# In-projection of a hybrid diffusion layer: TensorE keeps the order of the source instead of the scheduler's

## The chip, the cores and the metric

The kernel runs on one core of a Trainium2 chip. The metric is the time of one execution on the device in microseconds (us). The profile is one execution recorded by the hardware profiler; its times are counted from the first instruction of the program. PE is TensorE, DVE VectorE, ACT ScalarE, POOL GpSimd; SP is the queue that issues most DMA transfers. Each engine executes its own list of instructions strictly in the order of the program and waits on semaphores for the others.

## The reference

One layer of a backbone over 1024 latent tokens and 256 context tokens, width 1024, in float32. Cut to what matters:

```python
px = modulate(rms_norm(x, norm1_w), sh1, sc1) @ w_in       # latent, 1024 tokens
pc = modulate(rms_norm(ctx, norm1_w), csh1, csc1) @ w_in   # context, 256 tokens
# group A, gated DeltaNet on the first columns: short conv + SiLU on q, k, v; l2-normalised q, k;
# per chunk: decay, m = strict_lower((k beta) k^T * decay), a_mat = I + m, triangular solves with a_mat,
# then a scan over the chunks, forward and backward
# group B, neighbourhood attention: RMSNorm on q, k; 8 x 16 window keys and all context keys, one softmax
x = x + g1 * (concat([dn_x, na_x]) @ w_out)
x = x + g2 * swiglu(modulate(rms_norm(x, norm2_w), sh2, sc2), w_ffn_in, w_ffn_out)
```

The in-projection (`@ w_in`) with all that can already be done from its results (conv, norms, inverses of the chunks' triangular matrices) is the stage of this case. It lies at about 60 to 580 us of the span; attention and the scan follow up to about 815 us, then the output projection and the FFN.

## The kernel before

Every product with a large weight is taken in three passes of a split type: operands are divided into a high part (`whi`, `hh`) and a low part (`wlo`, `hl`), and high x high, high x low and low x high are summed in PSUM.

The stage works through a list of 24 **jobs**, each a block of 128 output columns for all tokens (`Block`, line 402, 8 k-tiles of 9 or 6 matmuls) or a wider one per token tile (`Wide`, lines 585 and 603, 24 matmuls a tile). The order of the jobs is k0, k1, k2, k3, z1, nk0, nk1, nk2, z0, nk3, nq0, nq1, nq2, q0, q1, q2, q3, nv0, v0, nv1, v1, v2, v3, nq3. (k, q, v, z belong to DeltaNet; nk, nq, nv to the neighbourhood attention.) k0 and k1 run before the loop that is changed.

The loop of lines 1032 to 1087 is a software pipeline written by hand. In turn n it issues the matmuls of job n; between them, step by step, the end of job n-2 (`finish`: transposes at line 524, products k k^T or q k^T at line 546); after them the copy of job n out of PSUM (`evac`: lines 435 to 458, with the convolution on DVE), the norm of job n-1 (`norm`: line 489 or 483) and the SiLU or square of job n. The weights of job n+1 are loaded at the start of turn n (line 195) and split by ACT (line 199) and POOL (line 200).

Beside that run two **background** generators, one step per k-tile or two per token tile:

- `block_inverses` (lines 806 to 892): decay tables (801), log-decays (837), 32 transposes to bring the 32 x 32 blocks on partitions (856), then on DVE 30 dependent pairs of multiply (866) and add (868) that invert all blocks in the tile `N`, then 32 transposes back (878) with copies by ACT (880), transposes and scalings on DVE (886, 889) and stores to `x_d` (888, 891).
- `preps` (898 to 1008): ten rounds, one for each position of the scan, each for both directions: decay products on POOL (`rg`, 938), matmuls 948 and 949, exp on ACT (952), products on DVE (955, 960), matmuls 967, copy 970, then three dependent steps of matmul 978 and copies on DVE (980) and ACT (981); diagonal blocks are copied by POOL (958, `y`) and ACT (942, `fx`) out of `xc`, which SP loads from `x_d` (922); results are stored by SP (990). Two rounds are in work at a time. The first two rounds are issued early; the other eight are issued once all q jobs are finished.

A third generator, `modulation` (lines 204 to 243), runs from job nq0 on and adds up the adaLN rows (232, 234) with four matmuls at line 219 for each of four parts. After job nv1, SP issues 64 transfers that rearrange the values (`vw_d`, line 1082).

What sets the order: the source only says in which order instructions are written. When the program is built, a scheduler decides for each engine, from a model of durations, which of the instructions that are ready in its model goes next, earlier written ones first; tiles get their buffers in the same pass. A block under `tc.manual_schedule(engines=...)` keeps the written order on the named engines; the other engines are still ordered by the scheduler. The kernel already has such a block for PE, DVE and ACT around the part before the loop.

Of the kernel before, what the change touches and what calls it, by code (L numbers as in the profile page):

```python
# [16 lines left out]
PSUM = bass.MemoryType.PSUM  # L17
DRAM = bass.MemoryType.DRAM

D, L, CT, T = 1024, 1024, 256, 1280  # L20
KT = 8
# [7 lines left out]
BLKS = [0, 8, 24, 32]  # L29
# [59 lines left out]
def hybrid(ctx, tc, a, dbg):  # L89
    nc = tc.nc  # L90
    pe, act, dve, pool, sp = nc.tensor, nc.scalar, nc.vector, nc.gpsimd, nc.sync

    def pools(stack, name, side=None, bufs=1, **kw):
        if side:
            kw["side"] = side
        return stack.enter_context(tc.tile_pool(name=name, bufs=bufs, reuse_waits="tile", **kw))
# [16 lines left out]
    middle = ctx.enter_context(ExitStack())  # L113
# [33 lines left out]
    nv_d = dram.tile([T, 512], F32, name="nv_d", tag="nv_d")  # L147
    nq_d = dram.tile([NAH, 2, ND, L], F16, name="nq_d", tag="nq_d")
    nk_d = dram.tile([2, NAH, ND, T], F16, name="nk_d", tag="nk_d")
    vw_d = dram.tile([128, 4, 4, 4, 128], F32, name="vw_d", tag="vw_d")  # L150
# [24 lines left out]
    bg = Background()  # L175
# [74 lines left out]
    attn = ctx.enter_context(ExitStack())  # L250
    psum = []
# [122 lines left out]
    with ExitStack() as bs:  # L374
# [4 lines left out]
        early = ExitStack()  # L379
# [362 lines left out]
        late = ExitStack()  # L742
# [153 lines left out]
        done = set()  # L896
# [113 lines left out]
        jobs = first + [Block("k", 2), Block("k", 3), Wide("z", 1, zp)]  # L1010
        inv = len(jobs)
        jobs += [Block("nk", i) for i in range(3)] + [Wide("z", 0, zp), Block("nk", 3)]
        jobs += [Block("nq", i) for i in range(3)] + [Block("q", 0)]
        turn = len(jobs)
        jobs += [Block("q", i) for i in (1, 2, 3)]
        later = len(jobs)
        values = later + 2
# [3 lines left out]
        def blk(n):  # L1021
            return jobs[n] if 0 <= n < len(jobs) and isinstance(jobs[n], Block) else None

        bg2 = Background()
# [4 lines left out]
        first[1].evac()  # L1029
        first[0].norm()  # L1030
        first[1].silu()
        for n in range(2, len(jobs) + 2):
            j = jobs[n] if n < len(jobs) else None
            if n == inv:
                early.close()
                psum.append(bs.enter_context(tc.tile_pool(name="psa", bufs=1, space=PSUM)))
                bg.add(block_inverses())
                bg.add(preps())
            if n == len(jobs) - 1:
                bg.drain()  # L1040
                bg2.drain()
                late.close()
                sp1 = pools(middle, "sp1", "left")
                fill = attention(pools(attn, "nw", "left", 2))
                next(fill)
            if n + 1 < len(jobs):
                jobs[n + 1].prefetch()
            fin = blk(n - 2) if n - 2 not in done else None
            fin = fin.finish() if fin else iter(())
            nrm = blk(n - 1)  # L1050
            if isinstance(j, Wide):
                for t, _ in enumerate(j.tiles()):
                    next(fin, 0)
                    if t == 4 and nrm:
                        nrm.norm()
                        for _ in fin:
                            pass
                        fin = nrm.finish()
                        done.add(n - 1)
                        nrm = None  # L1060
                    if n < turn:
                        bg.step(2)
                    if n >= turn:
                        bg.step(2)
            elif j:
                for k in range(KT):
                    j.mm([k])
                    if k >= 3:
                        next(fin, 0)
                    bg.step(1)  # L1070
                    if n > inv + 4:
                        bg2.step(1)
                j.evac()
            for _ in fin:
                pass
            done.add(n - 2)
            if isinstance(j, Wide) and n == values:
                vlat = nv_d[CT:].rearrange("(r c) d -> r c d", c=64)
                for cb in range(4):
                    for ch in range(4):  # L1080
                        for r in range(4):
                            sp.dma_start(vw_d[r * 32:r * 32 + 32, :, cb, ch],
                                         vlat[4 * ch + r, BLKS[cb]:BLKS[cb] + 32].rearrange("c (h d) -> c h d", d=128))
            if nrm:
                nrm.norm()
            if isinstance(j, Block):
                j.silu()

        dve.tensor_scalar(SQ, SQ, EPS, None, op0=OP.add)
        rsqrt(RQ, SQ, RQ2)  # L1090
# [226 lines left out]
    nrm = pools(early_u, "nrm", "left")  # L1317
# [11 lines left out]
    class Stream:  # L1329
# [67 lines left out]
        def next(self, n=2):  # L1397

            while len(self.got) < n:
                self.make()  # L1400
            out = [self.got.pop(0) for _ in range(n)]
            return out
# [21 lines left out]
    with ExitStack() as os_:  # L1424
        late = Background()
# [60 lines left out]
    with ExitStack() as us:  # L1486
# [91 lines left out]
        late = Background()  # L1578
# [170 lines left out]
```

## Time and profile before

| | us |
|---|---|
| time, median of 3 runs | 1555.27 (1553.62 to 1555.58) |
| time of the profiled execution | 1559.04 |
| its span, first to last instruction | 1556.6 |
| PE busy in the span | 1480.3 (95%) |
| PE busy from 60 to 580 us | 486.7 of 520 |

Busy time is a union of the times in which an engine's instructions ran. An engine can be busy and yet slow: the granted clock of PE is given separately. In a row of the timeline the columns are start, length, engine, line, operation, output and inputs with shapes, how many instructions were merged, and in brackets the idle time of the engine before it with what ended it. A matmul's length is its latency; in a stream the next one starts before it ends.

### The profile page before, as it was taken

To read this page: it belongs to the slowest core of one execution; us is meant where nothing else is said; L and a number is where in the kernel's file an instruction comes from. 1 tells how busy PE (TensorE), PEld (TensorE's weight loads), DVE (VectorE), ACT (ScalarE), POOL (GpSimd) and SP (SyncE) were. 2 spreads that over 40 slices of the span, in tenths; PEclk is the share of its full clock that TensorE was granted. 3 is DMA by queue.
4 is the path that set the end of the run, shared out by engine and by line. 5 is a ranking of instruction groups with operands and counts; after the bars stand their busy time and mean duration, and the time that the engine had idled before them with its cause. 6 is when DMAs were issued, how large, how long until landed. Compare 5 with 4: busy or idle time off the path is not lost. (4 is left out here: it accounts for less than half of the span.)

```text
span 1556.6 us, 23940 instructions
## 1 busy us (share of the span) xinstructions
PE 1480.3 (95%) x8702; PEld 1237.2 (79%) x8702; DVE 987.5 (63%) x1712; ACT 723.6 (46%) x1400; POOL 238.2 (15%) x286
## 2 busy tenths in 40 slices
PE   6999899999989987999899999999999999999998
PEld 3788787679888766887787878888888888888887
DVE  5774496674254755667786559856565656689652
ACT  5442553664343455665774256333333333454440
POOL 1154501633353320111210000000000000000000
PEclk9999999999999999999999999999999999999999
DMA  9274221677355568898737601633322224698742
GB/s 389 61 220 126 72 76 61 185 227 220 122 173 158 167 190 251 280 279 254 224 109 234 236 34 50 230 107 105 106 102 102 102 101 156 227 380 285 239 147 81
DMA packets 202423, 267.35 MB, mean 172 GB/s; under 512 B 16833, under 2 KB 112577, under 8 KB 201281
## 3 DMA queue, kind: packets, MB, share of 16 engines
q1 hardware_dynamic: 196688, 261.07, 51.5%
q10 hardware_dynamic: 5616, 4.76, 0.9%
q8 instruction: 68, 1.11, 0.3%
q14 instruction: 51, 0.41, 0.1%
HBM read 201.02 MB, written 68.94 MB: 173 GB/s over the span
## 5 line engine op out<-in xcount | busy, mean ns | idle before, releaser
L402 PE MATMUL blk<-hh,whi 128*128 128x512 f32 (+1 forms) x410 | 121.3, 390 | 1.4 <-ACT kk L547 1.4
L1387 ACT CAST uhi<-wq 128x512 fp32r<-128x512 f32 x101 | 61.0, 622 | 132.0 <-issue 84.6
L1387 ACT CAST uhi<-ws 128x512 fp32r<-128x512 f32 x91 | 53.9, 621 | 146.5 <-PE ps L1326 92.6
L402 PE MATMUL blk<-hh,wlo 128*128 128x512 f32 (+1 forms) x410 | 116.7, 378 | 0.6 <-POOL wlo L200 0.6
L402 PE MATMUL blk<-hl,whi 128*128 128x512 f32 (+1 forms) x410 | 115.6, 377 | 0.3 <-DVE hl L688 0.3
L1388 DVE TENSOR_TENSOR ulo<-wq,uhi 128x512 fp32r<-128x512 f32 x101 | 67.6, 688 | 58.8 <-ACT uhi L1387 32.5
L1326 PE MATMUL ps<-hT,uhi 128*128 128x512 f32 x336 | 103.6, 390 | 0.0
L1326 PE MATMUL ps<-lT,uhi 128*128 128x512 f32 x336 | 103.5, 389 | 0.0
L1326 PE MATMUL ps<-hT,ulo 128*128 128x512 f32 x336 | 103.5, 389 | 0.0
L1326 PE MATMUL ps<-hB,uhi 128*128 128x512 f32 x288 | 89.2, 391 | 0.6 <-ACT hB L1501 0.6
L1326 PE MATMUL ps<-lB,uhi 128*128 128x512 f32 x288 | 88.8, 389 | 0.4 <-DVE lB L1502 0.4
L1326 PE MATMUL ps<-hB,ulo 128*128 128x512 f32 x288 | 88.7, 389 | 0.0
L585 PE MATMUL blk<-zhi,hh 128*128 128x256 f32 (+1 forms) x288 | 84.5, 294 | 1.1 <-ACT kk L547 1.1
L402 PEld LDWEIGHTS blk<-hh,wlo 128*128 128x128 f32 x410 | 72.2, 191 | 15.4 <-POOL wlo L200 0.9
L402 PEld LDWEIGHTS blk<-hl,whi 128*128 128x128 f32 x410 | 72.4, 192 | 14.7 <-DVE hl L688 0.8
L585 PE MATMUL blk<-zhi,hl 128*128 128x256 f32 (+1 forms) x288 | 83.1, 288 | 0.0
L402 PEld LDWEIGHTS blk<-hh,whi 128*128 128x128 f32 x410 | 69.1, 191 | 16.4 <-issue 4.0
L585 PE MATMUL blk<-zlo,hh 128*128 128x256 f32 (+1 forms) x288 | 81.6, 283 | 0.0
L304 DVE CUSTOM_DVE_ANT_0 bt<-sc,bt 128x640 f32<-128x640 f32 x64 | 52.6, 822 | 34.6 <-PE sc L302 12.9
L1326 PEld LDWEIGHTS ps<-hT,ulo 128*128 128x128 f32 x336 | 63.1, 188 | 13.2
L1326 PEld LDWEIGHTS ps<-lT,uhi 128*128 128x128 f32 x336 | 63.1, 188 | 13.1
L1326 PEld LDWEIGHTS ps<-hT,uhi 128*128 128x128 f32 x336 | 62.9, 188 | 12.9
(360 smaller groups left out, 3645.9 us busy)
## 6 DMA issues: line engine op xcount, KB each, us to landing
wq<-w_fo SPq DMA_DIRECT2D x99, 256.0 KB, 4.3
wq<-w_gu SPq DMA_DIRECT2D x88, 256.0 KB, 2.8
wad<-wa SPq DMA_DIRECT2D x64, 256.0 KB, 3.9
bt<-rpb SPq DMA_DIRECT2D x64, 192.0 KB, 3.8
t_d<-g SPq DMA_DIRECT2D x22, 512.0 KB, 3.5
fr<-t_d SPq DMA_DIRECT2D x44, 256.0 KB, 5.1
f_d<-g SPq DMA_DIRECT2D x33, 256.0 KB, 2.1
fr<-f_d SPq DMA_DIRECT2D x33, 256.0 KB, 4.3
```

The source lines that it names most:

```text
L304: dve.tensor_tensor_reduce(bt, sc[:, u * 640:u * 640 + 640], bt, -1.0, 3.0e38, OP.add, OP.min, m[:, 0:1])
L402: pe.matmul(o, ww[:, k], xx[k][:, s], start=k == 0 and j == 0, stop=k == KT - 1 and j == 2)
L585: pe.matmul(p[:, :c1 - c0], x[k][:, s], ww[:, k, c0:c1], start=k == 0 and j == 0, stop=k == KT - 1 and j == 2)
L1326: pe.matmul(o, w[wi][:, k], x[xi][:, k], start=first and k == 0 and j == 0, stop=k == n - 1 and j == 2, skip_group_check=True)
L1387: act.copy(hi, self.raw[key])
L1388: dve.tensor_tensor(lo, self.raw[key], hi.bitcast(F32), OP.subtract)
```

## The change

The loop over the jobs is put under a manual schedule for PE. The body is the same, one level deeper, so line numbers behind line 1031 grow by one.

```diff
         first[1].silu()
-        for n in range(2, len(jobs) + 2):
-            j = jobs[n] if n < len(jobs) else None
-            if n == inv:
...
+        with tc.manual_schedule(engines={mybir.EngineType.PE}):
+            for n in range(2, len(jobs) + 2):
+                j = jobs[n] if n < len(jobs) else None
+                if n == inv:
...
+                if nrm:
+                    nrm.norm()
+                if isinstance(j, Block):
+                    j.silu()
```

The same instructions are issued, on the same tiles. On PE they stand in the written order inside the loop. ACT, DVE, POOL and SP are still ordered by the scheduler, now around a PE whose order is given.

More of the change, by code (lines that the diff above doesn't have):

```diff
@@ L1031, in hybrid @@
         first[1].silu()
-        for n in range(2, len(jobs) + 2):
-            j = jobs[n] if n < len(jobs) else None
-            if n == inv:
[L1035 to L1068, printed above, removed]
-                        next(fin, 0)
[L1070 to L1087, printed above, removed]
@@ new lines, in hybrid @@
+        with tc.manual_schedule(engines={mybir.EngineType.PE}):
+            for n in range(2, len(jobs) + 2):
+                j = jobs[n] if n < len(jobs) else None
+                if n == inv:
+                    early.close()
+                    psum.append(bs.enter_context(tc.tile_pool(name="psa", bufs=1, space=PSUM)))
+                    bg.add(block_inverses())
+                    bg.add(preps())
+                if n == len(jobs) - 1:
+                    bg.drain()
+                    bg2.drain()
+                    late.close()
+                    sp1 = pools(middle, "sp1", "left")
+                    fill = attention(pools(attn, "nw", "left", 2))
+                    next(fill)
+                if n + 1 < len(jobs):
+                    jobs[n + 1].prefetch()
+                fin = blk(n - 2) if n - 2 not in done else None
+                fin = fin.finish() if fin else iter(())
+                nrm = blk(n - 1)
+                if isinstance(j, Wide):
+                    for t, _ in enumerate(j.tiles()):
+                        next(fin, 0)
+                        if t == 4 and nrm:
+                            nrm.norm()
+                            for _ in fin:
+                                pass
+                            fin = nrm.finish()
+                            done.add(n - 1)
+                            nrm = None
+                        if n < turn:
+                            bg.step(2)
+                        if n >= turn:
+                            bg.step(2)
+                elif j:
+                    for k in range(KT):
+                        j.mm([k])
+                        if k >= 3:
+                            next(fin, 0)
+                        bg.step(1)
+                        if n > inv + 4:
+                            bg2.step(1)
+                    j.evac()
+                for _ in fin:
+                    pass
+                done.add(n - 2)
+                if isinstance(j, Wide) and n == values:
+                    vlat = nv_d[CT:].rearrange("(r c) d -> r c d", c=64)
+                    for cb in range(4):
+                        for ch in range(4):
+                            for r in range(4):
+                                sp.dma_start(vw_d[r * 32:r * 32 + 32, :, cb, ch],
+                                             vlat[4 * ch + r, BLKS[cb]:BLKS[cb] + 32].rearrange("c (h d) -> c h d", d=128))
+                if nrm:
+                    nrm.norm()
+                if isinstance(j, Block):
+                    j.silu()
```

## Prediction

> **What bounds the kernel now.** I read the page first: PE is busy for 95% of the span, and the stage that is changed is one of its less full parts. Then busy time of the engines in stretches of that stage, then who PE waited for in it.
>
> ```profile
> 60.00:224.80 164.80, 155.17 (x982) 135.57 (x981) 108.23 (x149) 80.38 (x138) 66.07 (x59) 1.00 0.39 120
> 224.80:255.80 31.00, 27.40 (x142) 22.84 (x140) 30.03 (x32) 6.49 (x10) 2.55 (x1) 0.99 0.18 52
> 255.80:311.50 55.70, 52.45 (x295) 39.41 (x295) 29.28 (x31) 35.21 (x63) 29.07 (x36) 0.88 0.51 164
> 311.50:400.00 88.50, 86.92 (x535) 76.74 (x534) 47.36 (x63) 41.42 (x61) 25.22 (x22) 0.98 0.68 201
> 400.00:513.70 113.70, 102.95 (x831) 90.67 (x830) 51.44 (x58) 48.08 (x106) 54.16 (x53) 0.97 0.52 159
> 513.70:533.10 19.40, 19.40 (x101) 16.24 (x99) 13.08 (x17) 4.50 (x6) 2.31 (x8) 1.00 0.82 265
> 533.10:565.00 31.90, 28.87 (x249) 21.87 (x249) 19.73 (x29) 17.94 (x40) 14.00 (x21) 1.00 0.31 105
> ```
>
> The columns are stretch, length, then busy time (instructions) of PE, PE's weight loads, DVE, ACT and POOL, then PE's granted clock, the share of the DMA engines and GB/s. PE fills most of each stretch, so what delays it there lengthens the kernel. One stretch is full on two engines: from 224.8 to 255.8, DVE is busy for 30.0 of 31.0 us while PE has 27.4 us of work. That DVE work is the inversion of the blocks in `N`:
>
> ```profile
> L868 DVE TENSOR_TENSOR N<-N,tt 80x120 f32<-80x120 f32 (+14 forms) x30 | 27.5, 916 | 0.9
> L866 DVE TENSOR_TENSOR tt<-N 80x120 f32<-80x120 f32 (+14 forms) x30 | 27.5, 915 | 4.7 <-ACT N L858 3.8
> L497 DVE SCALAR_TENSOR_TENSOR cacc<-cacc,qkw,cr 128x1280 f32<-128x1280 f32 x2 | 3.1, 1547 | 0.3 <-ACT cr L494 0.3
> L503 DVE TENSOR_TENSOR hl<-cacc,hl 128x1280 f16<-128x1280 f32 x2 | 3.0, 1480 | 0.0
> ```
>
> These groups of DVE, asked for 193.9 to 256.7 us, add up to 61 of 62.8 us: 30 dependent pairs back to back, with two norms between them. Nothing that PE does brings `N` forward. PE's waits from 60 to 580 us:
>
> ```profile
> PE pr L967 <- DVE y L980: 5.6, 3, 2.6
> PE pr L967 <- DVE kk L955: 4.8, 4, 3.8
> PE m L878 <- DVE N L872: 3.6, 1, 3.6
> PE pr L948 <- POOL rg L938: 3.2, 3, 1.8
> PE m L489 <- ACT cr L490: 2.9, 2, 1.5
> ```
>
> Each line is total, times and longest. All are small: the scheduler gave PE other matmuls while results of DVE and POOL were on their way.
>
> **The change, part by part.** The programs as built show how the order on PE moves. Around the transposes back out of `N` (line 878), rows of one kind merged by me:
>
> ```
> before: L585 x59 | L402 x116 | L878 x2 | L402 x3 | L878 x6 | L402 x4 | L878 x8 | L402 x2 | L878 x8 | L402 x2 | L878 x8 | L402 x4 | ...
> after:  L585 x48 | L878 x8 | L585 x24 | L878 x16 | L402 x9 | L878 x8 | L402 x36 | L948 x2 | L949 | L948 x2 | L949 | L402 x9 | L967 x8 | ...
> ```
>
> The scheduler had put 24 matmuls of z0 and 116 of nk3 and nq0 ahead of the first transpose; the source has it before them. The order of DVE's 60 inversion steps is the same in both.
>
> *A, the displaced work.* Where PE stands, what it did before the transpose, and when `N` is ready:
>
> ```profile
> 224.82 0.28 PE L585 MATMUL blk<-zhi,hh 128*128 128x264 f32 x1
> ...
> 227.72 0.74 PE L402 MATMUL blk<-hh,whi 128*128 128x256 f32 x3
> ```
> ```profile
> 226.50:252.20 25.70, 24.48 (x116) 20.04 (x116) 1.00 0.22 62
> ```
> ```profile
> 255.62 0.38 DVE L868 TENSOR_TENSOR N<-N,tt 80x232 f32<-80x232 f32 x1
> ```
> ```profile
> 255.83 0.53 PE L878 MATMUL m<-cst,N 80*128 80x80 f32 x2 [3.63 <-DVE N L872]
> 256.10 1.20 PE L402 MATMUL blk<-hl,whi 128*128 128x512 f32 x2
> ```
>
> After the change PE meets the transpose at 224.8 and stands still until `N` comes, about 29 to 31 us instead of 3.63. The matmuls behind it are ready (the next one ran 0.3 us after the transpose) but cannot pass. The work that filled the time, 27.4 us by the second row of the first table (2.9 us of z0, 24.5 of line 402), is still to be done. One thing comes back: POOL's split of a weight, which waits for PE to free a buffer, will not run beside the inversion. It did, and one DVE step took three times its neighbour:
>
> ```profile
> 242.57 2.55 POOL L200 TENSOR_TENSOR wlo<-wraw,whi 128x1024 fp32r<-128x1024 f32 x1 [40.88 <-ACT whi L199]
> ```
> ```profile
> 241.88 0.98 DVE L866 TENSOR_TENSOR tt<-N 80x792 f32<-80x792 f32 x1
> 242.89 3.07 DVE L868 TENSOR_TENSOR N<-N,tt 80x792 f32<-80x792 f32 x1
> ```
>
> 3.07 less 0.98 is 2.1 us. A is 27.4 - 2.1 = **+25.3** (25.3 to 27.4).
>
> *B, from `N` to the first two rounds of preps.* Before, this is how the chain went:
>
> ```profile
> 265.14 1.51 DVE L886 STREAM_TRANSPOSE ut<-WK 128x1280 f32<-128x1280 f32 x1 [8.51 <-ACT WK L880]
> ...
> 273.97 1.50 DVE L886 STREAM_TRANSPOSE ut<-WK 128x1280 f32<-128x1280 f32 x1
> ```
> ```profile
> 277.66 2.85 POOL L200 TENSOR_TENSOR wlo<-wraw,whi 128x1024 fp32r<-128x1024 f32 x1 [16.12 <-ACT whi L199]
> 280.46 0.99 POOL L912 MEMSET fx<- 128x512 f32 x2
> ...
> 284.29 1.03 POOL L938 TENSOR_TENSOR rg<-GL,cst 128x512 fp32r<-128x512 f32 x1
> ```
> ```profile
> 284.37 0.51 PE L948 MATMUL pr<-rg,mr 128*128 128x512 f32 x1 [1.83 <-POOL rg L938]
> ```
>
> The first matmul of the preps comes 28.5 us after the first transpose. Afterwards only 32 transposes (0.15 us apart), 24 z0 and 45 matmuls of line 402 lie between, about 4.8 + 2.9 + 9 us, so PE arrives some 17 us after `N`. The chain is shorter too: POOL's wlo and DVE's norms no longer stand in it. But the last transposes come later, behind 24 z0 and 9 others (4.7 us), and the stores that must land before `rg` gets its memory stay. I estimate `rg` at 24 us after `N` (not below 20, not over 28), a wait of 7. The whole stretch idled 3.25 us before (55.70 less 52.45). B is **+4** (0 to +8). What PE does in the wait's place is nothing; nk3 and nq0 then lie between the preps instead of nq1 and nq2.
>
> *C, the first turn.* In turn 2 the third bank and the first transposes were put off:
>
> ```profile
> 72.21 0.39 PE L402 MATMUL blk<-hl,whi 128*128 128x512 f32 x1
> ...
> 80.39 1.25 PE L524 MATMUL m<-cst,cacc 128*128 128x128 f32 x10
> ```
> ```profile
> 78.12 1.28 ACT L465 ACTIVATE cacc<-cacc 128x1280 f32<-128x1280 f32 x1
> ```
>
> In the written order PE waits at about 69 for the bank, which was in use at 72.21, and 34 matmuls of some 0.19 us later reaches the first transpose at about 78.5, 0.9 us before ACT's SiLU ends at 79.4. That is some 3 us lost, of which later waits on DVE and ACT (line 489 among them) swallow two. C is **+1** (0 to +3).
>
> *D, the rounds behind the 64 transfers.* Here the scheduler had put 98 matmuls of line 402 ahead of line 978:
>
> ```profile
> 486.95 29.73 SPq L1082 DMA_DIRECT2D vw_d<-nv_d  x46
> ```
> ```profile
> 520.49 2.67 POOL L958 COPY y<-xc 32x128 f32<-32x128 f32 x8 [9.11 <-DMA y_d<-y]
> ```
> ```profile
> 513.74 0.83 PE L402 MATMUL blk<-hh,whi 128*128 128x256 f32 x3
> ```
>
> SP issues one transfer in 0.65 us, so stores and loads of the preps queue behind them until 516.7, and POOL's copies end at 523.2. The written order has 18 matmuls (3.5 us) after 513.74 and then line 978: a wait from 517.2 to 523.2, 6.0 us at the same places. It is long enough to lower the clock (below), 3.4 us more. What the scheduler paid for the delay, 3.0 us idle from 533.1 to 565, goes. D is 6.0 + 3.4 - 3.0 = **+6.4** (0 to +9.4).
>
> *The clock.* After the 3.63 us of idle time:
>
> ```profile
> 252.00:256.00 4.00, 0.37 (x2) 0.17 (x2) 3.72 (x9) 0.00 (x0) 0.00 (x0) 0.89 0.00 0
> 256.00:260.00 4.00, 4.00 (x15) 3.22 (x16) 0.56 (x3) 2.20 (x4) 0.83 (x1) 0.50 0.00 0
> 260.00:264.00 4.00, 4.00 (x27) 3.58 (x26) 0.00 (x0) 2.70 (x6) 1.54 (x1) 0.76 0.24 71
> ```
>
> Lost clock: 4 x (0.11 + 0.50 + 0.24) = 3.4 us. A already pays one such drop before and one after, however long the wait, so it adds nothing there; B has one on both sides too. [...]
>
> *E, fewer changes of kind.* Three matmuls of line 402 take 0.09 us more behind line 967, which is in full float32, than behind line 585 (0.83 at 513.74, 0.74 at 227.72). By the built programs PE goes from one kind to another 42 times less. E is **-3** (-4 to 0). From 577 to 650 us the order on PE shifts by up to 50 places, behind that it is the same; ACT gets three more table loads beside other work. Both: 0 (-2 to +2).
>
> **The sum.** 25.3 + 4 + 1 + 6.4 - 3 = +33.7 us on the profiled execution of 1559.04 (span 1556.6), 1592.7. The median of the runs is 3.8 lower, so I predict **1589 us**.
>
> **The rivals.** *The lag is made up later.* PE idles 1.6, 10.8 and 3.0 us in the stretches from 311.5 to 400, 400 to 513.7 and 533.1 to 565. If the results waited for there come at fixed times, a late PE waits less. Against it: line 967 waits for products of line 955, which start from PE's own 948. All of it recovered is -15.4: 1574 us. Chance 0.14.
>
> *The other side: not slower.* That holds if the loop's second half is bound by the chain of the preps and not by PE, so that the displaced matmuls fall into its holes. Idle time after 255.8 is 3.3 + 15.4, lost clock 0.12 x 55.7 + 0.02 x 88.5 + 0.03 x 113.7 = 11.9: 30.6 us in all. It decides from 27.4 us recovered on; with all of it and without D and B the time is 1555.3 + 25.3 + 1 - 3 - 30.6 = 1548 us. Against it: the eight later rounds stand behind q3 in the written order, so their chain starts late with PE. Chance 0.04.
>
> *More waits.* Two rounds, not one, meet the transfers of line 1082, and the adaLN sums (line 219), which start 50 us later, are late as well: another 9.4 and some 5 us, 1603 us. Chance 0.10.
>
> *No effect* is excluded by the built order but for 0.01. My forecast has 0.71.
>
> **How the numbers follow.** The range is 1571 to 1604: the low end is the recovery, the high end the sum of the upper bounds (27.4 + 8 + 3 + 9.4 + 2 = 49.8, 1605) and the third rival. No change within 0.2% (3.1 us, about what a measurement can tell) has 0.02: slower by more than that 0.94, faster 0.04.
>
> **What would show it.** A: line 878 waits 28 to 31 us for `N`, in one piece, from about 225. B: line 948 waits 4 to 11 us near 273. D: line 978 waits for POOL's `y` near 550. The eight later rounds start about 30 us later than 410. I am wrong if `N` is ready much before 253, if PE passes line 878 sooner, or if the start of attention is not 25 to 45 us later than 579.

## The result, and the profile after

The changed kernel takes 1613.38 us (median of 4 runs, 1610.17 to 1617.19) against 1554.44 us of the kernel before on the same chip. The ratio is 1.0374, with a 95% interval of 1.0357 to 1.0391: it is slower by some 59 us, where 34 were predicted, and the time lies above the predicted range. The span of the profiled execution is 1612.8 us against 1556.6, and PE's mean granted clock 0.967 against 0.983.

First the busy time in stretches of the stage, in the columns used above. The stretches answer to those of before: where PE reaches the transposes, where it leaves them, and the later rounds of the preps.

```profile
60.00:240.00 180.00, 159.36 (x983) 138.06 (x981) 110.97 (x151) 83.56 (x140) 65.72 (x59) 0.96 0.36 110
240.00:265.90 25.90, 0.02 (x1) 0.05 (x1) 24.97 (x30) 0.64 (x2) 0.00 (x0) 0.60 0.14 36
265.90:340.00 74.10, 64.48 (x376) 50.93 (x377) 19.58 (x23) 32.70 (x64) 31.85 (x52) 0.89 0.42 135
340.00:444.00 104.00, 103.30 (x592) 88.92 (x591) 53.80 (x71) 49.98 (x66) 18.02 (x7) 0.97 0.56 169
444.00:557.00 113.00, 101.87 (x825) 89.75 (x823) 48.10 (x53) 47.47 (x105) 52.92 (x53) 0.95 0.51 157
557.00:637.00 80.00, 63.07 (x414) 50.08 (x413) 42.54 (x58) 30.72 (x54) 18.39 (x34) 0.89 0.50 157
```

From 240.0 to 265.9 PE has no work at all beside DVE's inversion. That is the wait that the prediction's step A named. But two more stretches lose time. To the same place in the work (983 instructions of PE against 982) PE needs 180.0 us from 60 on, where it needed 164.8: 15 us are gone before the wait begins. And the last stretch has 17 us of idle time at a clock of 0.89. PE's waits from 60 to 660 us (total, times, longest) say for whom:

```profile
PE m L878 <- DVE N L872: 25.9, 1, 25.9
PE m L489 <- ACT cr L490: 13.0, 4, 7.4
PE pr L978 <- DVE y L980: 12.5, 4, 5.3
PE pr L948 <- POOL rg L938: 6.0, 3, 5.6
PE pr L967 <- DVE kk L955: 5.4, 3, 4.5
PE pr L978 <- POOL y L958: 4.6, 2, 4.0
```

The longest ones in PE's timeline, in order of time:

```profile
188.46 2.08 PE L489 MATMUL m<-cr,cst 128*128 128x512 f32 x2 [7.35 <-ACT cr L490]
...
265.88 0.51 PE L878 MATMUL m<-cst,N 80*128 80x80 f32 x2 [25.92 <-DVE N L872]
...
290.15 0.80 PE L948 MATMUL pr<-rg,mr 128*128 128x512 f32 x1 [5.63 <-POOL rg L938]
...
568.20 0.78 PE L978 MATMUL pr<-y,kk 128*32 128x32 f32 x16 [4.04 <-POOL y L958]
...
596.60 1.07 PE L978 MATMUL pr<-y,kk 128*32 128x64 f32 x16 [3.47 <-DVE y L980]
...
617.94 1.49 PE L978 MATMUL pr<-y,kk 128*32 128x96 f32 x16 [5.27 <-DVE y L980]
```

Lines 878, 948 and 978 (for POOL's `y`) are the waits of steps A, B and D. The first row, and the two waits of line 978 for DVE, stand in no step of the prediction; a third wait of line 978 for DVE, 3.42 us, ends at 491.31.

How late the kernel is at four marks puts a size on each place:

| mark | before, us | after, us | later by |
|---|---|---|---|
| first step of DVE's inversion (line 866) | 193.98 | 205.02 | 11.0 |
| first matmul of nv0 (line 585) | 372.61 | 416.78 | 44.2 |
| last norm of the stage (line 489) | 576.52 | 635.92 | 59.4 |
| end of the span | 1556.6 | 1612.8 | 56.2 |

So 11 us are lost before the inversion starts, 33 from there to nv0, and 15 in the late turns; attention and what follows give 3 back. (PE itself is 15 us late at line 878, because it also waits 2.35 and 1.34 us at line 489 while the inversion runs; `N` is what it waits for next, so these two cost nothing more.)

**What stood in front of the inversion.** ACT's timeline of the changed kernel, around 184 us:

```profile
177.25 0.38 ACT L839 ACTIVATE W<-m 128x256 f32<-128x256 f32 x1
184.32 1.05 ACT L199 CAST whi<-wraw 128x1024 fp32r<-128x1024 f32 x1 [6.69 <-DMA wraw<-w_nqk]
185.27 1.35 ACT L435 ACTIVATE cacc<-blk 128x256 f32<-128x256 f32 x3
186.64 1.28 ACT L490 ACT_TABLE_LOAD   x1
187.93 1.05 ACT L490 ACTIVATE cr<-m,bias 128x256 f32<-128x256 f32 x2
```

and of the kernel before, at the same work:

```profile
174.47 0.38 ACT L839 ACTIVATE W<-m 128x256 f32<-128x256 f32 x1
176.81 1.36 ACT L435 ACTIVATE cacc<-blk 128x256 f32<-128x256 f32 x3 [1.96 <-PE blk L402]
178.19 1.28 ACT L490 ACT_TABLE_LOAD   x1
...
182.16 1.05 ACT L199 CAST whi<-wraw 128x1024 fp32r<-128x1024 f32 x1
```

The change does not touch ACT. But the scheduler, which orders ACT around a PE whose order is now given, put the cast of the next weights (line 199) ahead of the copy out of PSUM (line 435) and of the norm (line 490). The cast has to wait for its weights: SP issued that load at 179.92, and ACT stood still for 6.69 us with work behind the cast that was ready (PE's last matmul for the copies of line 435 ended at 179.82). The norm came at 187.93 instead of 179.49, PE waited for it, and the whole chain to `N` started late. In these rows the copies behind the cast did not pass it: it starts at 184.32, they at 185.27.

### The profile page after: what moved, and what is told of

Its sections match the earlier page's. It is cut to its first block, busy times and chain, and to the rows that moved or that the text cites. A ratio compares the mean times of both kernels' runs of the same rounds, so it can differ in the third digit from the quotient of the medians.

```text
span 1612.8 us, 23958 instructions
## 1 busy us (share of the span) xinstructions
PE 1485.0 (92%) x8702; PEld 1240.1 (77%) x8702; DVE 981.3 (61%) x1712; ACT 729.2 (45%) x1403; POOL 230.3 (14%) x286
## 5 line engine op out<-in xcount | busy, mean ns | idle before, releaser
L402 PE MATMUL blk<-hh,whi 128*128 128x512 f32 (+1 forms) x410 | 125.5, 404 | 7.0 <-DVE cacc L444 2.7
L402 PE MATMUL blk<-hh,wlo 128*128 128x512 f32 (+1 forms) x410 | 112.7, 375 | 0.0
L1389 DVE TENSOR_TENSOR ulo<-wq,uhi 128x512 fp32r<-128x512 f32 x101 | 67.7, 687 | 59.4 <-ACT uhi L1388 35.0
L402 PEld LDWEIGHTS blk<-hl,whi 128*128 128x128 f32 x410 | 73.9, 196 | 15.2 <-DVE hl L688 0.8
```

The lines of the kernel that those rows point to most:

```text
L402: pe.matmul(o, ww[:, k], xx[k][:, s], start=k == 0 and j == 0, stop=k == KT - 1 and j == 2)
L1389: dve.tensor_tensor(lo, self.raw[key], hi.bitcast(F32), OP.subtract)
```

## The experiments

All are variants of the changed kernel unless said otherwise. The ratio is to the kernel before, run on the same chip beside each. The median of the kernel before moves from 1554.44 to 1556.03 between these sessions, so differences between runs of different sessions carry an uncertainty of 1 to 2 us, and more where a kernel's own runs spread.

| run | median, us | ratio (95% interval) |
|---|---|---|
| e1, weights' load later in turn 6 | 1605.46 | 1.0303 (1.0270 to 1.0336) |
| e2, transposes later | 1600.65 | 1.0275 (1.0237 to 1.0312) |
| e3, both | 1588.09 | 1.0200 (1.0170 to 1.0230) |
| e4, hand-kept to turn 16 | 1596.42 | 1.0252 (1.0223 to 1.0282) |
| e5, e3 and preps later | 1580.54 | 1.0156 (1.0134 to 1.0177) |
| e6, hand-kept from turn 17 only | 1571.64 | 1.0092 (1.0074 to 1.0110) |
| e7, hand-kept from turn 5 | 1610.46 | 1.0344 (1.0327 to 1.0362) |
| e8, e5 hand-kept to turn 16 | 1566.20 | 1.0061 (1.0036 to 1.0086) |
| e9, e6 with `y` copied by ACT | 1555.42 | 0.9993 (0.9975 to 1.0011) |
| e10, before with `y` copied by ACT | 1545.41 | 0.9925 (0.9897 to 0.9952) |
| e11, e8 from turn 5, preps later still | 1562.89 | 1.0044 (1.0020 to 1.0067) |
| e12, the whole loop by hand, with all remedies | 1566.83 | 1.0067 (1.0032 to 1.0101) |

**e1: is it ACT's list?** Turn 6 loads the next weights behind its evacuation. PE's order stays as it is.

```diff
-                if n + 1 < len(jobs):
+                if n + 1 < len(jobs) and not (n == 6):
                     jobs[n + 1].prefetch()
...
-                    j.evac()
+                    j.evac(); n == 6 and jobs[n + 1].prefetch()
```

> The changed kernel with one step moved: in turn 6 the load of the next block's weights (nk2: L195, its cast L199 on ACT and its subtraction L202 on POOL) is written behind the evacuation of that turn's block instead of at the head of the turn. TensorE's order stays the changed kernel's, instruction for instruction; on ACT the cast L199 comes behind L435 and L490. Theory (ACT's list, not TensorE's, made the stall at 188 us): the wait of 7.35 us for L490 at 188.46 falls to 1 to 2 us, the first L866 comes 8 to 11 us earlier than 205.0, all later work moves up by as much with the wait in front of L878 unchanged at 24 to 28 us; 1602 to 1606 us. Rival (the third L489 waits for a free bank whatever ACT does, or what is won is given back at the wait for N): the wait stays above 5 us or L878 waits longer by what was won; 1611 to 1615 us.

It took 1605.46 us, 7.9 less than the changed kernel. PE's wait fell from 7.35 to 1.48 us:

```profile
183.46 1.13 PE L489 MATMUL m<-cr,cst 128*128 128x512 f32 x2 [1.48 <-ACT cr L490]
```
```profile
180.26 1.36 ACT L435 ACTIVATE cacc<-blk 128x256 f32<-128x256 f32 x3 [1.77 <-PE blk L402]
181.64 1.28 ACT L490 ACT_TABLE_LOAD   x1
...
185.61 1.05 ACT L199 CAST whi<-wraw 128x1024 fp32r<-128x1024 f32 x1
```

The inversion began at 197.6 instead of 205.0, and the wait in front of line 878 kept its length (26.4 us): all moved up as a whole. The theory holds: 8 us of the loss come from ACT's list and not from PE's.

**e2, e3 and e5: the two waits of the inverse's chain.** e2 puts empty steps into the background work ahead of the transposes, e3 adds e1's edit, and e5 puts ten more steps ahead of the first prep.

```diff
-                U = WK.rearrange("p d u i -> p (d u) i")
+                U = WK.rearrange("p d u i -> p (d u) i"); yield from [1] * 16
...
-                todo = list(range(NCH))
+                todo = list(range(NCH)); yield from [1] * 10     # e5 only
```

> The changed kernel with sixteen empty steps in the background work ahead of the inverse's transposes, so that the first L878 stands some 26 to 28 us of block matmuls later in TensorE's order, about where the scheduler had put it. Theory (terms A and B: TensorE runs dry at L878 because the source puts the transposes ahead of work that could run): the 25.9 us at L878 fall below 1 us and the 5.6 us at L948 below 2 us; the preparations begin up to 25 us of TensorE work later but have slack; 1580 to 1586 us. Rival (the displaced steps are missed at the end: what does not fit in front of the last turn is drained there with nothing beside it): gain at 270 us, but 10 to 25 us of it lost between 560 and 660; 1592 to 1608 us.

> The two edits of the runs before together (weights' load behind the evacuation in turn 6, sixteen empty steps ahead of the inverse's transposes). Theory (the two losses stand one behind the other and add): 8 to 11 us below the run with the late transposes alone, 1570 to 1577 us. Rival (they overlap: with N ready 10 us earlier the transposes were late already): no more than 2 us below it.

e2 took 1600.65 us: 13 won where the theory asked for 27 to 33. Its four executions spread from 1594.56 to 1603.72; the profiled one is the fastest, 20.0 below that of the changed kernel. PE's timeline of e2 shows that the first wait went and the second doubled:

```profile
266.50 0.45 PE L878 MATMUL m<-cst,N 80*128 80x80 f32 x2 [1.85 <-DVE N L872]
...
296.94 0.79 PE L948 MATMUL pr<-rg,mr 128*128 128x512 f32 x1 [10.67 <-POOL rg L938]
```

This is neither the theory nor its rival, which expected the loss at the end of the stage. In the changed kernel the way from the first transpose to POOL's `rg` was partly covered by what lay between the transposes; with those moved closer together, 24 matmuls of line 402 are left behind the last of them. Why `rg` cannot come sooner stands in POOL's timeline of e3, which took 1588.09 us, 12.6 less than e2 by the medians and 4.9 by the profiled executions. So e1's gain of 7.9 adds, as far as e2's spread lets one tell, and the times that e3's theory named (1570 to 1577) are missed because e2's were:

```profile
290.03 1.04 POOL L938 TENSOR_TENSOR rg<-GH,cst 128x512 fp32r<-128x512 f32 x1 [12.22 <-DMA x_d<-ut]
```

POOL waits for the stores of the inverse to memory: the buffers of the preps lie where those tiles were. That makes some 30 us from line 878 to line 948 (260.6 to 291.1) that PE must fill.

> The kernel with both edits (e3) and ten more empty steps ahead of the first preparation, so that some 66 block matmuls instead of 24 stand between the last inverse transpose L878 and the first L948 in TensorE's order (the scheduler had some 60). In e3 TensorE waits 10.7 us there for POOL's first rg, which comes only when x_d is written. Theory (the way from N over U, ut, x_d and rg to L948 takes about 30 us whatever TensorE does, and the source gives it too little cover): the 10.7 us fall below 2 us and nothing of it comes back behind; 9 to 13 us below e3, 1575 to 1580 us. Rival (the next link is late in its turn, kk and xc read from memory): another wait of 5 us or more at L967 or L978 in front of 330 us, 1584 to 1590 us.

e5 took 1580.54 us, 7.5 below e3, between theory and rival. Its timeline of PE:

```profile
258.90 0.45 PE L878 MATMUL m<-cst,N 80*128 80x80 f32 x2 [2.31 <-DVE N L872]
...
295.73 0.50 PE L948 MATMUL pr<-rg,mr 128*128 128x512 f32 x1 [0.49 <-POOL rg L938]
...
306.46 3.40 PE L967 MATMUL pr<-fx,kk 128*128 128x128 f32 x16 [4.43 <-DVE kk L955]
```

The 10.7 us fell to 0.5, and 4.4 us came at the next link of the same chain. From e1 to e5, 24.9 us are won by nothing but matmuls that stand ahead of the waits instead of behind them.

**e7: the first turns.** The order is kept from turn 5 on only. The edit is shown against the kernel before.

```diff
+        keep = ExitStack()
         for n in range(2, len(jobs) + 2):
-            j = jobs[n] if n < len(jobs) else None
+            j = jobs[n] if n < len(jobs) else None; n == 5 and keep.enter_context(tc.manual_schedule(engines={mybir.EngineType.PE}))
...
+        keep.close()
```

> The changed kernel with the hand-kept order begun at turn 5 (nk0) instead of at turn 2: TensorE's order is that of before through turn 4. It measures term C, the first turns. Theory (C is the lag of 2.5 us that stands from 100 to 180): the waits at 72 and 92 us are those of before, all else as in the changed kernel, 1608 to 1613 us. Rival (the start decides more: the ACT list that made the stall at 188 is a result of the first turns' order): that stall is gone too, 1598 to 1604 us.

e7 took 1610.46 us, 2.9 less than the changed kernel (4.5 less when each is set against the kernel before on its own chip). The waits at 72 and 92 us (2.7 and 1.3) are gone, the one at 188 is 5.79 instead of 7.35. The first turns cost some 3 us, little more than these runs differ by, and ACT's stall does not come from them: in e7 too ACT waits 6.58 us with the cast of line 199.

**e4 and e6: the late turns.** e4 ends the hand-kept order at turn 17, e6 begins it there, by the same edit with other bounds.

> The changed kernel with the hand-kept order ended at turn 17 (the first nv tile): TensorE's order is the changed kernel's through turn 16 and the scheduler's from there. Theory (the lag that grows from 45 us at 540 to 57 us at 640 is made by the source's order of the late turns): the waits for the copies of y (L978, 3.5 and 5.3 us at 597 and 618) and for the first preparation's POOL work at 568 (4.0 us) fall under 1.5 us each, and the lag stays at 43 to 46 us; 1598 to 1603 us. Rival (the late waits come from the preparations' running 45 us later against the 64 transfers of vw_d and the convolutions on DVE, whatever TensorE's order): lag at the end as before, 1610 to 1615 us.

> The kernel before with the source's order kept from turn 17 on only (the complement of e4): TensorE's order is that of before through turn 16, the changed kernel's behind it. Theory (the late loss is made by the order alone: the source puts L978 closer behind the copies of y than DVE's convolutions allow): waits at L978 for DVE's L980 of 3 to 6 us appear twice between 535 and 580, and 1567 to 1573 us. Rival (it needs the preparations to run 45 us late, which they do not do here): 1553 to 1558 us.

e4 took 1596.42 us, 17.0 less than the changed kernel and a little below its theory's range; e6 took 1571.64, inside its theory's range and 15.6 more than the kernel before. The two agree: the order of the late turns costs some 16 us, whether the stage is late there or not. The timeline of PE in e6, whose stage is not late:

```profile
523.74 0.89 PE L978 MATMUL pr<-y,kk 128*32 128x32 f32 x16 [4.42 <-POOL y L958]
...
552.10 1.07 PE L978 MATMUL pr<-y,kk 128*32 128x64 f32 x16 [3.46 <-DVE y L980]
...
574.83 1.50 PE L978 MATMUL pr<-y,kk 128*32 128x96 f32 x16 [5.27 <-DVE y L980]
```

They are the waits of the changed kernel to 0.4 us. What DVE does ahead of the copies that PE waits for, in the changed kernel:

```profile
587.21 8.92 DVE L458 SCALAR_TENSOR_TENSOR cacc<-cr,cw,cacc 128x254 f32<-128x254 f32 x8
596.16 0.29 DVE L980 COPY y<-pr 32x128 f32<-32x128 f32 x1
...
612.50 4.85 DVE L458 SCALAR_TENSOR_TENSOR cacc<-cr,cw,cacc 128x255 f32<-128x255 f32 x6
617.37 0.42 DVE L980 COPY y<-pr 32x256 f32<-32x256 f32 x1
```

and in the kernel before, at the first and second step of the last round:

```profile
559.11 0.29 DVE L980 COPY y<-pr 32x128 f32<-32x128 f32 x1
559.43 0.48 DVE L458 SCALAR_TENSOR_TENSOR cacc<-cr,cw,cacc 128x254 f32<-128x254 f32 x1
559.83 0.79 DVE L454 TENSOR_SCALAR cacc<-cr,cw 128x1024 f32<-128x1024 f32 x1
561.12 0.42 DVE L980 COPY y<-pr 32x256 f32<-32x256 f32 x1 [0.50 <-PE pr L978]
```

A copy of 0.29 us stands behind 8.92 us of a value block's convolution. In the last round, 6.1 us of convolution (611.43 to 617.35) stand between the copies of the first and the second step, where the kernel before has 1.3: DVE's list was made anew as well. And PE has less to do meanwhile. The scheduler had put 98 matmuls of line 402 ahead of the round of step D; the source has 18 there, 22 (lines 402 and 524) between the steps at 588.55 and 596.60, and none between those at 612.06 and 617.94.

**e9 and e10: is it DVE's queue?** One direction's copies go from DVE to ACT, in e6 (e9) and in the kernel before (e10).

```diff
-                        dve.tensor_copy(y[0][blk[0], :, cols[0]], ps[0][blk[0], :, :32 * n])
+                        act.copy(y[0][blk[0], :, cols[0]], ps[0][blk[0], :, :32 * n])
```

> e6 (source's order on TensorE from turn 17 on only) with the copies L980 of the first direction's y moved from DVE to ACT, where those of the second (L981) already are; TensorE's order from turn 17 on stays that of e6. Theory (the late loss is DVE working off a block's convolutions, up to 8.9 us of L458 in a row, in front of a copy of 0.3 to 0.5 us that TensorE waits for): the waits of 3.4, 3.5 and 5.3 us at L978 fall below 1.5 us each, 1559 to 1565 us. Rival (each step of the preparation is simply too short for its copy on any engine; ACT has L450 and L465 in front of it): waits of 2 to 5 us remain, now for ACT, 1567 to 1574 us.

> The kernel before with the same edit, the copies L980 on ACT instead of DVE: what the edit is worth where the scheduler orders TensorE, to set beside e9, and a try at a faster kernel. Theory: the 5.6 us at L967 and the 2.4 us at L978 that wait there for L980 go and little comes in their place, 1549 to 1554 us. Rival (the scheduler had laid matmuls over those waits, and ACT is later with the second copy): 1555 to 1560 us.

e9 took 1555.42 us, 16.2 less than e6; e10 took 1545.41, 10.6 less than the kernel before. Both lie 3.6 us below their theories' ranges. In e9 the two waits of line 978 for DVE are gone, but others stand in PE's timeline:

```profile
445.77 1.06 PE L978 MATMUL pr<-y,kk 128*32 128x64 f32 x14 [5.60 <-ACT y L981]
...
522.29 0.97 PE L978 MATMUL pr<-y,kk 128*32 128x32 f32 x16 [6.31 <-POOL y L958]
```

The first of these stands where e6 waited 3.43 us for DVE (446.60); the second was 4.42 us in e6. So the waits at 552 and 575 in e6 were DVE's queue, and in place of the one at 447 PE now waits for ACT. But the edit helps the scheduler's order too, and set against e10 the late turns' order still costs 10.0 us (1555.42 less 1545.41): with little work of PE between the steps, whichever engine is late makes PE wait. Of the 16 us, some 6 hang on the copies' being on DVE. The gain in e10 was larger than expected. Only 7.9 of its 13.9 us of span are won by the start of attention (570.0 against 577.9); the other 6 come later, where among others a wait of 5.3 us for DVE (line 1206 for line 1195) is gone. Why it is gone stays open.

e10 is the fastest kernel of this study, 0.75% below the kernel before (0.48 to 1.03%).

**e8, e11 and e12: does the account close?**

> e5 with the hand-kept order ended at turn 17: the weights' load behind the evacuation in turn 6, the inverse's transposes and the first preparation later, the late turns in the scheduler's order. Theory (ACT's cast, the two waits of the inverse's chain, and the late turns are the whole loss but for the first turns' 2.5 us): 1556 to 1561 us. Rival (the hand-kept order from 340 to 480 costs a further 4 us or more, or the lower clock behind the waits has another cause): 1564 to 1572 us.

> e8 with the hand-kept order begun at turn 5 (undoes C) and four more empty steps ahead of the first preparation, fourteen in all (against the 4.3 us at L967 that e8 shows at 307 us). Theory (the rest of e8, 10 us above before, is C's 3 us and the waits of the first preparations with the lower clock behind them): 1556 to 1561 us. Rival (keeping the source's order in turns 5 to 16 costs something that no single wait shows): 1563 to 1567 us.

> The changed kernel, with the source's order kept over the whole loop as in the change, and the remedies of the runs before: the weights' load behind the evacuation in turn 6, sixteen empty steps ahead of the inverse's transposes and fourteen ahead of the first preparation, the copies L980 on ACT. Theory (what the change lost is places in the list and one engine's queue, not the keeping of the order itself; e5's 1580.5 less the 16 us that the copies brought between e6 and e9, less 2 for the four further steps): 1560 to 1566 us. Rival (the two gains overlap, or ACT, now with every copy, is late in the early turns too): 1568 to 1576 us.

e8 took 1566.20 us, 10 above the kernel before and in its rival's range. Its trace puts 10.9 us of loss between the first transpose and nv0 (127.5 us, from 259.0 to 386.5, against 116.6), 7.0 of them idle time of PE. e11, which also gives the first turns back to the scheduler and moves the preps four steps further, took 1562.89, just below its rival's range. So 52 of the 59 us are found by name; 6.9 us (0.20 to 0.67% of the time) remain. e11 still has waits of 3.4 to 3.5 us at lines 219 and 967 near 297 and 330, and waits more at line 489 (6.7 us against 2.9); which of them makes the rest was not separated. Its executions spread from 1558.61 to 1571.80, and the profiled one, 1558.97, has the span of the kernel before (1556.6), so most of the 6.9 us does not stand in that trace. e12 keeps the written order in the whole loop, as the change does, and took 1566.83, a little above the theory's range and 11.4 us above the kernel before: some 47 us of the loss went by moving work in the source and a copy to another engine, with the hand-kept order left in place.

## Why the prediction was right in its direction and wrong in its size

**A and B, the inverse's chain: right.** PE stood at line 878 for 25.92 us in one piece (predicted: 28 to 31) and at line 948 for 5.63 (predicted: 4 to 11). Both came later than named, since PE and `N` were late: 240.0 to 265.9 instead of 225 to 255. The two steps were put at 29.3 us; between the marks on both sides 33 were lost, and e2, e3 and e5 gave back 24.9 beyond e1 with a wait of 4.4 still in place.

**C, the first turns: the size was near, the step behind it failed.** The turns cost 3 us (e7) instead of 1. But C says that later waits, those of line 489 among them, swallow what is lost. Line 489 became the second largest wait of the stage. The prediction read the orders of PE and of DVE's inversion in the changed program, and took ACT's order to be harmless beside three table loads; it took the time at which `N` is ready from the trace of before. "Nothing that PE does brings `N` forward" is true, but other things could put it back, and ACT's cast did so by 8 us (e1). This term was missing from the sum, and it has no place in the range.

**D, the late turns: the right place, less than half of the size.** D was 6.4 us, from the wait for POOL's `y` alone: 4.04 us came at 568, where 6.0 were named near 550. Its cause was the named one: SP issues the transfers of `vw_d` until 562.8, and POOL's copies start at 566.88, after 8.83 us of waiting for a DMA. The late turns cost some 16 us (e4, e6). The prediction priced one of the places where the scheduler had slid matmuls ahead of line 978, and none for DVE's copies, which stand in DVE's list behind the convolutions (3.42, 3.47 and 5.27 us, each with a lower clock behind it: 0.50 from 492 to 497, from 597 to 599 and from 618 to 623).

**E, the changes of kind: not told.** No run separates its 3 us.

**The sum.** Between the marks the span grew by 56.2 us where the terms gave 33.7. Of the 22.5 between them, 10.0 came ahead of the inversion (11.0 against C's 1), 3.9 around it (33.2 against 29.3) and 8.8 in the late turns (15.2 against 6.4); E's forecast gain of 3 lies in these stretches and cannot be told apart, and 3.2 came back behind the stage. So the sum failed above all in the missing term for ACT's list and in the size of D. The prediction's own sign says the same: attention was to start 25 to 45 us later than 579, and it starts 59.4 later, at 638.69. The clock's 3.4 us in D was counted over whole stretches, 0.4 of it while PE stood still.

**The rivals.** *The lag is made up later* did not come: 44.2 us at nv0 became 59.4 at the end of the stage. *Not slower* fell by the same numbers. *More waits* had the direction, but other culprits: no wait of line 219 stands among the changed kernel's larger ones, and the 64 transfers of `vw_d` need not meet a late round, as e6 shows with a stage that is on time. The upper end of the range, 1604, was about the sum of the upper ends of the terms that had been found (1605 by the prediction's own figures; its low end, 1571, lies 3 us under the 1574 that it is said to be). It held nothing for a term that had not.

## What to carry to other kernels

Fixing the order of PE made the scheduler order ACT and DVE anew here (6.69 us of ACT's standing still with the cast, 6.1 us of convolution on DVE between two copies where 1.3 stood before). Where the order of one engine is fixed, read the new list of every engine for an instruction fed by a transfer that now stands ahead of one that the fixed engine waits for. Where a scheduler's order is replaced by the source's, look for every place where it had slid work ahead of a wait, not only the largest, and give the source that cover (steps of other work ahead of the consumer) or take the producer off a busy queue. A range made from the bounds of the terms that one has found is too narrow by those that one has not.

## What the hardware did that was not expected

PE's clock fell after shorter waits than the 3.63 us from which the prediction took its drop (3.47 us in the changed kernel, 2.31 us in e5), and its return took a varying time. PE in stretches of 4 us, with busy time, granted clock, DMA share and GB/s, in the changed kernel:

```profile
266.00:270.00 4.00, 3.74 (x19) 0.50 0.00 0
270.00:274.00 4.00, 3.93 (x25) 0.72 0.00 0
...
596.00:600.00 4.00, 3.40 (x23) 0.57 0.01 4
600.00:604.00 4.00, 4.00 (x23) 1.00 0.00 0
616.00:620.00 4.00, 2.06 (x18) 0.50 0.01 4
620.00:624.00 4.00, 4.00 (x11) 0.52 0.69 239
```

and in e5, behind the wait of 2.31 us at 258.90:

```profile
258.00:262.00 4.00, 2.69 (x14) 0.94 0.00 0
262.00:266.00 4.00, 4.00 (x21) 0.63 0.00 0
```

The clock that is lost to work is counted here as PE's busy time in a stretch times what the clock lacks to 1. After the 25.92 us it is 3.74 x 0.50 + 3.93 x 0.28 = 3.0 us. After the 3.63 us of the kernel before, from the prediction's rows, it is 0.37 x 0.11 + 4.00 x 0.50 + 4.00 x 0.24, also 3.0: in these two cases the long wait cost no more clock than the short one, as step A assumed. After 3.47 us at 596.60 it is 3.40 x 0.43 = 1.5 us, after 5.27 us at 617.94 it is 2.06 x 0.50 + 4.00 x 0.48 = 3.0. The way back differed. In stretches of 1 us the clock reads 0.53 from 599 to 600 and 1.00 in the next, which begins 3.4 us after PE starts again at 596.60. After the other three waits it took nearly twice as long, about 6 us (an estimate from such stretches): 0.87 from 272 to 273, behind the start at 265.88, 0.58 from 623 to 624, behind that at 617.94, and in the kernel before 0.54 from 261 to 262, behind that at 255.83, each time with 1.00 in the next stretch. In e5 the clock fell, to 0.63 from 262 to 266, behind 2.31 us of idle time, eight transposes of line 878 and 0.41 us more of idle time among them.
